# A two-layer hybrid mixer on one core: the Fourier branch takes its position transform first and in half, and unused columns move where operand rows begin

## The chip, the cores and the metric

The kernel runs on one core of a Trainium2 chip. The metric is the device time of one execution in microseconds. Beside it stands one profiled execution, whose span runs from its first instruction to its last. Lower is better.

## The reference

Two layers work on two sequences of 256 tokens with 1024 channels: the latent tokens and the context tokens. Each layer normalises and modulates its input, multiplies it by one wide input matrix, and feeds three token mixers. Branch A is a Fourier mixing, branch B a gated delta rule run forwards and backwards over chunks, branch C a differential attention. Each branch is projected back to 1024 channels and gated, the three are summed, one output matrix follows, and then a squared-ReLU MLP of width 4096. Layer 0 carries both sequences; in layer 1 only the latent tokens go on after the keys, values and states, so most of its products have 256 columns where those of layer 0 have 512.

The part that the change is about is this:

```
def fourier_mix(u):                      # u: (batch, t, 512)
    uf = u.reshape(b, t, 4, 128)         # 4 groups of 128 channels
    y = fft2(uf, axes=(1, 3), norm='ortho').real
    return y.reshape(b, t, 512)
y_f = fourier_mix(h @ w_in[:, 0:512]) @ w_f
```

With C and S the cosine and sine matrices, the real part for one group is C_pos u C_ch - S_pos u S_ch. The cosine over positions is even and the sine is odd, so position 256 - t repeats position t up to a sign.

## The kernel before

**Products.** All large products take float32 operands split in two rounded halves (`split`, L257: a ScalarE copy gives the high half, a VectorE subtraction the low half) and are three matmuls each (`mm3`, L241): high by high, low by high, high by low. `gemm` (L246) runs `mm3` over eight blocks of 128 input channels into one PSUM bank: a chunk of 128 x 1024 weights is stationary, block by block, and the tokens move, 512 or 256 columns at a time. A chunk is thus 24 matmuls. `load_w` (L226) fetches a chunk by a SyncE DMA, copies it on ScalarE and subtracts on VectorE (`whi`, `wlo`).

**Layer.** `mixer` (L448) calls in order: `front` (modulation of the input, and products that start while it runs), `dn_pair(0)` (q, k, v products of two delta-rule heads and their convolution), `fnet` (the Fourier branch), `scores` and `values` (attention inputs), `branch` for the Fourier projection and its gate, the attention, the chain of head pair 0, and then the same for pair 1, the other gates and projections, and the merge. `accumulate` (L1116) does the output matrix (`C_WO`) and the second MLP matrix. `mlp` (L1156) writes the squared hidden values as the pair `a`.

**Order of the work.** The delta-rule chain of small dependent matmuls is written out after the products, and `weave.chain()` places its instructions among those already written, by their planned TensorE time. Beyond that, instructions are put on each engine in order of priority as they become ready, so a product that stands later in the code can run ahead where a PSUM bank is free. There are eight banks, two each under the tags `pg`, `pa`, `pc` and `pd`; the chain uses `pc` and `pd`. Within `fnet` a product may use `pg` alone.

**`fnet` before (L880).** Channel-major: for each of the four groups, one chunk gives u (128 channels x n tokens; n is 512 in layer 0, 256 in layer 1). It is split, each tile of 128 tokens is stationary against the 128 x 256 table `cc` (both channel transforms), the result z is split, and then z is stationary against the position table `ct` (256 columns), over two token tiles and over cosine and sine. The result is split into `yb`. Group 0 of layer 0 is computed already in `front0` (L1280).

**Where operand rows begin.** A tile's columns lie one after another in each partition. The rows of the operands below are 1024 or 2048 bytes apart, so all rows of one operand begin at the same byte modulo 512. From the allocation:

| moving operand | columns of a matmul | bytes mod 512, layer 0 | layer 1 |
|---|---|---|---|
| `hh`, `hl` (input of all products) | 512 or 256 | 288, 288 | 288, 288 |
| `a0`, `a1` (MLP hidden values) | 512 (layer 0), 256 (layer 1) | 288, 352 | 480, 480 |
| `yh`, `yl` (Fourier, then attention output) | 512, 256 | 480, 480 | 480, 480 |
| `ydh`, `ydl` (delta-rule output) | 512, 256 | 128, 128 | 64, 64 |
| `ct`, `cc` (transform tables) | 256 | 224 | 128 |
| weight chunks `whi`, `wlo` | (128 when stationary) | 288 | 288 |

Of the kernel before, what the change touches and what calls it, by code (L numbers as in the profile page):

```python
# [30 lines left out]
NLVL = 7  # L31

# [47 lines left out]
def constants():  # L80
# [89 lines left out]
def body(tc, A, dbg=None):  # L170
# [12 lines left out]
    hh = [hp.tile([P, KT, T], F32R, name=t_) for t_ in ("hh", "hl")]  # L183
# [23 lines left out]
    def abank():  # L207
        return bank("pa")
# [43 lines left out]
    def step_of(jobs, k, t0, n, order=range(KT), X=hh):  # L252
# [72 lines left out]
    def lambdas(pool):  # L325
        lamv = wp.tile([P, 1024], F32, tag="raw", name="raw", bufs=4)[:, 0:R_END - R_LAM]
        nc.gpsimd.dma_start(lamv, A["rows"][R_LAM:R_END].partition_broadcast(P))
        lamv = lamv.rearrange("p (a b c) -> p a b c", a=DEPTH, b=4)
        for l in range(DEPTH):
            lj = pool.tile([P, 2, 64], F32, name=f"lj{l}")  # L330
# [104 lines left out]
    def modulate(l, x, r, a, base, s, k, pool, eng=V):  # L435
        sl = slice(s * L, (s + 1) * L)
        t = pool.tile([P, L], F32, tag="mt", name="mt", bufs=3)
        hi, lo = hh[0][:, k, sl], hh[1][:, k, sl]
# [9 lines left out]
    def mixer(l, last, front):  # L448
# [3 lines left out]
        H = hh  # L452
# [427 lines left out]
        def fnet():  # L880
# [4 lines left out]
            cr = raw_tile(A["ct"])  # L885
            ct = [fp.tile([P, 1024], F32R, name=f"ct{i}") for i in range(2)]
            split(cr, ct[0], ct[1])
            ct = [c_.rearrange("p (k c) -> p k c", k=2) for c_ in ct]
            cc = [fp.tile([P, 256], F32R, name=f"cc{i}") for i in range(2)]
            split(raw_tile(A["kc"][:, K_CC:K_CC + 256], 256), cc[0], cc[1])  # L890
            nt = n // P
            for g in range(4):
                ps = product(("u", g), C_U + g, n)
                uh = [fp.tile([P, n], F32R, tag=f"uh{i}", name=f"uh{i}", bufs=2) for i in range(2)]
                split(ps[:, :n], uh[0], uh[1])
                z = [fp.tile([P, nt, 256], F32R, tag=f"z{i}", name=f"z{i}") for i in range(2)]
                for tt in range(nt // 2):
                    pz = abank()
                    for i in range(2):
                        t = 2 * tt + i  # L900
                        tk = slice(t * P, (t + 1) * P)
                        mm3(pz[:, i * 256:(i + 1) * 256], uh[0][:, tk], uh[1][:, tk], cc[0], cc[1], True, True)
# [561 lines left out]
```

## Time and profile before

| | |
|---|---|
| median of 3 runs | 1619.63 us (1617.7 to 1624.81) |
| the profiled execution's own time | 1620.69 us |
| its span | 1618.9 us |
| TensorE busy | 1541.4 us, 95% of the span, 10270 matmuls |
| VectorE busy | 1183.2 us, 73% |
| ScalarE busy | 738.9 us, 46% |
| granted TensorE clock, mean | 0.990 |

The busy time of TensorE (PE) is modelled from starts, since matmuls overlap, so the page alone doesn't tell how fast a stream of them runs. For that one takes the start of the first and the last matmul of an unbroken run and divides by their number. PEld is the weight load that goes ahead of each matmul; DVE is VectorE and ACT is ScalarE.

### The profile page before, as it was taken

How to read it: one execution, taken by the hardware profiler on the slowest of the kernel's cores; microseconds unless marked ns; L12 is line 12 of the kernel's file. 1: busy time of each engine (PE TensorE's matmuls, PEld its weight loads, DVE VectorE, ACT ScalarE, POOL GpSimd, SP SyncE). 2: the span in 40 equal slices, each digit the busy share in tenths (PEclk: the TensorE clock that was granted, in tenths of full speed). 3: DMA queues.
4: the chain of work that ended last, by engine and by line, in shares of the span. 5: the costliest groups of instructions: out<-in, count | busy, mean ns of one | idle time of the engine just before them, and what ended most of it. 6: DMA issues, size and time to landing. Idle time of an engine off the chain costs nothing.

```text
span 1618.9 us, 26446 instructions
## 1 busy us (share of the span) xinstructions
PE 1541.4 (95%) x10270; PEld 1327.9 (82%) x10270; DVE 1183.2 (73%) x2221; ACT 738.9 (46%) x1525; POOL 187.9 (12%) x196
## 2 busy tenths in 40 slices
PE   5889999999999999999999999899999999999997
PEld 2568888778787878788888888788988899999997
DVE  7686665767789867967767664876877885887765
ACT  3465543566542233422223233465547554555543
POOL 3420100011002103000000004211111102000001
PEclk9999999999999999999999999899999999999998
DMA  6522123211166635466656552231332125656662
GB/s 234 186 89 66 34 66 117 90 54 38 48 196 202 219 127 200 130 196 195 182 182 196 173 171 82 70 121 60 93 117 79 41 89 177 186 170 192 189 185 91
DMA packets 64462, 215.85 MB, mean 133 GB/s; under 512 B 7281, under 2 KB 12305, under 8 KB 64081
## 3 DMA queue, kind: packets, MB, share of 16 engines
q1 hardware_dynamic: 58178, 202.48, 39.8%
q10 hardware_dynamic: 5184, 7.21, 1.3%
q0 software_dynamic: 976, 4.48, 0.9%
q8 instruction: 80, 1.31, 0.3%
q14 instruction: 44, 0.36, 0.1%
HBM read 209.95 MB, written 4.20 MB: 132 GB/s over the span
## 4 chain that ended last, share of the span: by engine, by line
PE 73%; DVE 15%; ACT 5%; issue 3%; DMA 3%; POOL 0%; DVEq 0%; ACTq 0%; SPq 0%; POOLq 0%
PE pg L146 35%; PE pd L146 13%; PE pa L146 12%; PE pc L146 11%; DVE junk L319 3%; DVE cy L614 2%; DVE wlo L238 2%; DMA raw<-in_wt 2%; ACT whi L237 1%; DVE mt L440 1%; ACT sw L952 1%; PE pc L154 1%; PE pa L154 1%; DMA wv<-in_wt 0%; DMA x<-in_xin 0%
## 5 line engine op out<-in xcount | busy, mean ns | idle before, releaser
L238 DVE TENSOR_TENSOR wlo<-raw,whi 128x1024 fp32r<-128x1024 f32 x262 | 326.4, 1246 | 99.1 <-ACT whi L237 96.5
L237 ACT CAST whi<-raw 128x1024 fp32r<-128x1024 f32 x277 | 290.1, 1049 | 223.2 <-PE pg L146 79.7
L146 PE MATMUL pg<-hh,whi 128*128 128x512 f32 (+1 forms) x912 | 324.7, 356 | 1.8 <-DVE gt L876 1.8
L146 PE MATMUL pg<-hh,wlo 128*128 128x512 f32 (+1 forms) x912 | 323.9, 355 | 2.0 <-POOL wlo L238 1.5
L146 PE MATMUL pg<-hl,whi 128*128 128x512 f32 (+1 forms) x912 | 323.2, 354 | 0.0
L146 PEld LDWEIGHTS pg<-hh,whi 128*128 128x128 f32 x912 | 172.6, 189 | 23.7 <-issue 3.1
L319 DVE CUSTOM_DVE_ANT_0 junk<-raw,cb 128x1024 f16<-128x1024 f32 x128 | 160.4, 1253 | 41.8 <-DMA raw<-in_wt 38.2
L146 PEld LDWEIGHTS pg<-hh,wlo 128*128 128x128 f32 x912 | 172.7, 189 | 22.0 <-POOL wlo L238 1.8
L146 PEld LDWEIGHTS pg<-hl,whi 128*128 128x128 f32 x912 | 173.0, 190 | 20.7 <-issue 0.8
L417 POOL TENSOR_TENSOR acc<-acc,sq 128x256 f32<-128x256 f32 x36 | 38.9, 1088 | 596.3 <-ACT sq L415 596.3
L146 PE MATMUL pg<-a,whi 128*128 128x256 f32 (+1 forms) x416 | 102.0, 328 | 0.1
L614 DVE SCALAR_TENSOR_TENSOR cy<-cu,conv,cy 128x512 f32<-128x512 f32 (+1 forms) x96 | 75.7, 789 | 30.9 <-ACT cy L612 28.5
L146 PEld LDWEIGHTS pg<-a,whi 128*128 128x128 f32 x416 | 70.7, 188 | 8.4 <-DVE a L259 0.5
L860 ACT ACTIVATE gt<-pg 128x512 f32<-128x512 f32 (+1 forms) x44 | 21.6, 491 | 114.6 <-PE pg L146 100.8
L146 PE MATMUL pg<-a,wlo 128*128 128x256 f32 (+1 forms) x208 | 68.0, 327 | 0.0
L146 PE MATMUL pc<-a,whi 128*128 128x512 f32 (+1 forms) x224 | 57.2, 336 | 0.1
L146 PE MATMUL pd<-a,whi 128*128 128x256 f32 (+1 forms) x224 | 54.7, 328 | 0.0
L1186 DVE TENSOR_TENSOR mr<-mr 128x512 f32<-128x512 f32 (+1 forms) x64 | 35.4, 555 | 25.3 <-ACT mr L1185 25.2
L740 ACT CAST Um<-pd 128x512 f16<-128x512 f32 x56 | 34.1, 610 | 35.8 <-PE pd L146 35.3
L146 PE MATMUL pa<-a,whi 128*128 128x256 f32 (+1 forms) x208 | 50.0, 324 | 0.1
L146 PE MATMUL pa<-hh,whi 128*128 128x512 f32 (+1 forms) x128 | 48.3, 377 | 0.0
L146 PE MATMUL pa<-hl,whi 128*128 128x512 f32 (+1 forms) x128 | 48.1, 376 | 0.0
(435 smaller groups left out, 3675.3 us busy)
## 6 DMA issues: line engine op xcount, KB each, us to landing
raw<-in_wck SPq DMA_DIRECT2D x280, 512.0 KB, 3.6
raw<-in_wt SPq DMA_DIRECT2D x80, 512.0 KB, 3.6
wv<-in_wt SPq DMA_DIRECT2D x10, 512.0 KB, 4.2
wn<-in_wn SPq DMA_DIRECT2D x16, 192.0 KB, 3.8
x<-in_xin SPq DMA_DIRECT2D x4, 512.0 KB, 8.6
spill<-gt ACTq DMA_DIRECT2D x8, 256.0 KB, 4.0
cb<-crow POOLq DMA_DIRECT2D x2, 1024.0 KB, 5.8
merged<-spill ACTq DMA_DIRECT2D x8, 256.0 KB, 4.4
```

Of the source, the lines that this page charges most:

```text
L146: ins = self.pe.matmul(out, a, b, start=start, stop=stop)
L154: self.pe.transpose(out, a, ident)
L237: S.copy(hi, r)
L238: eng.tensor_tensor(out=lo, in0=r, in1=hi.bitcast(F32), op=ALU.subtract)
L319: V.tensor_tensor_reduce(out=junk, in0=r, in1=self.cb[:, v], scale=0.5, scalar=0.0, op0=ALU.mult, op1=ALU.add, accum_out=ada[l][:, n, v:v ...
L417: G.tensor_tensor(out=self.acc[s], in0=self.acc[s], in1=q, op=ALU.add)
L440: V.scalar_tensor_tensor(out=t, in0=x[s][:, k], scalar=gain, in1=r[s], op0=ALU.mult, op1=ALU.mult)
L614: V.scalar_tensor_tensor(out=y3, in0=u[:, 0:ns, j:j + L], scalar=conv[:, f, j:j + 1], in1=y3, op0=ALU.mult, op1=ALU.add)
L740: S.copy(uc_, pU.rearrange("p (d b c) -> p d b c", d=2, c=w_))
L860: S.activation(th, ps[:, :n], AF.Tanh, scale=0.5)
L952: S.copy(sw[b:b + 32], ps[b ^ 32:(b ^ 32) + 32, 0:L])
L1186: V.tensor_tensor(out=t, in0=t, in1=t, op=ALU.mult)
```

## The change

`fnet` works on token-major data. The four chunks of u's weights are laid out by input channel, so that now the tokens are stationary (128 of them) and 512 weight columns move; n/128 banks (4 in layer 0, 2 in layer 1) hold u for all groups at once. A unit is one group of one sequence: 8 in layer 0, 4 in layer 1. Two units at a time, `positions` multiplies u by a table of 256 columns that holds 129 cosines and 127 sines in place of 512 columns, and after a split `channels` applies cosine and sine of the channels to the two halves, with `cc` stationary and z moving (260 and 256 columns). The sine part is copied in reverse to the second half of y on ScalarE, VectorE subtracts it for positions 1 to 127 and adds it for their mirror images, and y is split into `yb`. In `front0` the chunk of u that was computed early is replaced by gate chunk (C_GF, 1).

The second part are columns that nothing uses. `hh` is made 48 columns wider and `hl` 80: layer 0 uses `hh` from column 0 and `hl` from column 80, layer 1 `hh` from column 48 and `hl` from 0. The two make 128 columns, 512 bytes, so what lies behind keeps its byte modulo 512. `pad` allocates 48 columns behind `yb` in layer 0 (its pool grows downwards), 40 and 104 columns ahead of `yd` in layers 0 and 1, and 112 ahead of `a1` in layer 0. By these sums rows begin at 288 for `hh`, `hl`, `a0`, `a1`, `yb` and `yd` in layer 0, and at 480 for all of them in layer 1. `lambdas` puts a scratch product into a weight buffer in place of two tiles of its own.

```
--- before.py
+++ after.py
+NC = L // 2 + 1
-    ct = np.concatenate([np.cos(a) / 16, -np.sin(a) / 16], axis=1).astype(np.float32)
-    ct = ct.reshape(2, P, 512).transpose(1, 0, 2).reshape(P, 1024)
+    ct = np.concatenate([np.cos(a[:, 0:NC]) / 16, np.sin(a[:, 1:NC - 1]) / 16], axis=1).astype(np.float32)
+    ct = ct.reshape(2, P, L).transpose(1, 0, 2).reshape(P, 2 * L)
+SHIFT = ((0, 48), (80, 0))
+PAD = {"y": (48, 0), "yd": (40, 104), "a": ((0, 112), (0, 0))}
+def pad(pool, w):
+    if w:
+        pool.tile([P, w], F32, name="pad")
-    hh = [hp.tile([P, KT, T], F32R, name=t_) for t_ in ("hh", "hl")]
+    hs = [[], []]
+    for t_, at_ in zip(("hh", "hl"), SHIFT):
+        t = hp.tile([P, KT * T + max(at_)], F32R, name=t_)
+        for l_ in range(DEPTH):
+            hs[l_].append(t[:, at_[l_]:at_[l_] + KT * T].rearrange("p (k c) -> p k c", c=T))
...
-            cr = raw_tile(A["ct"])
-            ct = [fp.tile([P, 1024], F32R, name=f"ct{i}") for i in range(2)]
-            split(cr, ct[0], ct[1])
+            ct = [fp.tile([P, 2 * L], F32R, name=f"ct{i}") for i in range(2)]
+            split(raw_tile(A["ct"], 2 * L), ct[0], ct[1])
...
-            for g in range(4):
-                ps = product(("u", g), C_U + g, n)
...
+            ps = [bank("pg") if t < 2 else bank("pa") for t in range(nt)]
+            for c in range(4):
+                w = [w_.rearrange("p k c -> p (k c)") for w_ in load_w(l, C_U + c)]
+                for i in range(2):
+                    k, cols = 2 * c + i, slice(512 * i, 512 * i + 512)
+                    for t in range(nt):
                         tk = slice(t * P, (t + 1) * P)
-                        mm3(pz[:, i * 256:(i + 1) * 256], uh[0][:, tk], uh[1][:, tk], cc[0], cc[1], True, True)
...
+                        mm3(ps[t], H[0][:, k, tk], H[1][:, k, tk], w[0][:, cols], w[1][:, cols], k == 0, k == KT - 1)
+            u = [fp.tile([P, nt, 512], F32R, name=f"u{i}") for i in range(2)]
+            for t in range(nt):
+                split(ps[t], u[0][:, t], u[1][:, t])
+            units = [(g, s) for g in range(4) for s in range(nseq)]
+            def positions(i):
+                pq = bank("pg").rearrange("p (a c) -> p a c", a=2)
+                for j, (g, s) in enumerate(units[i:i + 2]):
+                    gs = slice(g * P, (g + 1) * P)
                     for k in range(2):
+                        mm3(pq[:, j], u[0][:, 2 * s + k, gs], u[1][:, 2 * s + k, gs], ct[0][:, k], ct[1][:, k], k == 0, k == 1)
+                return pq
+            def channels(i, z):
+                pa_, pb_ = (abank()[:, :2 * w_].rearrange("p (a c) -> p a c", a=2) for w_ in (NC + 1, NC - 1))
+                mm3(pa_, cc[0][:, 0:P], cc[1][:, 0:P], z[0][:, :, 0:NC + 1], z[1][:, :, 0:NC + 1], True, True)
+                mm3(pb_, cc[0][:, P:2 * P], cc[1][:, P:2 * P], z[0][:, :, NC - 1:L], z[1][:, :, NC - 1:L], True, True)
+                y = fp.tile([P, 2, L], F32, tag="y", name="y")
+                sn = y[:, :, L - 1:NC - 1:-1]
+                S.copy(y[:, :, NC:L], pb_[:, :, NC - 2:0:-1])
+                S.copy(y[:, :, 0:NC:NC - 1], pa_[:, :, 0:NC:NC - 1])
+                V.tensor_tensor(out=y[:, :, 1:NC - 1], in0=pa_[:, :, 1:NC - 1], in1=sn, op=ALU.subtract)
+                V.tensor_tensor(out=sn, in0=pa_[:, :, 1:NC - 1], in1=sn, op=ALU.add)
+                g = units[i][0]
+                hi, lo = (t[:, g:g + 2] if last else t[:, g].rearrange("p (a c) -> p a c", a=2) for t in yb)
+                split(y, hi, lo)
+            pq = positions(0)
+            for i in range(0, len(units), 2):
+                z = [fp.tile([P, 2, L], F32R, tag=f"z{j}", name=f"z{j}") for j in range(2)]
+                split(pq, z[0], z[1])
+                if i + 2 < len(units):
+                    pq = positions(i + 2)
+                channels(i, z)
...
         yb = [yp.tile([P, 4, n], F32R, name=t_) for t_ in ("yh", "yl")]
+        pad(yp, PAD["y"][l])
...
+        pad(tp, PAD["yd"][l])
         yd = [tp.tile([P, 4, n], F32R, name=t_) for t_ in ("ydh", "ydl")]
...
+            a = []
+            for i in range(2):
+                if q == 0:
+                    pad(pool, PAD["a"][l][i])
+                a.append(pool.tile([P, KT, n], F32R, tag=f"a{i}", name=f"a{i}", bufs=2))
...
-                          lambda: job(("u", 0), load_w(0, C_U, pair(st, "wu"), G), "pa"),
+                          lambda: job((C_GF, 1), load_w(0, C_GF + 1, pair(st, "wu"), G), "pa"),
...
-        wck[l, C_U:C_U + 4] = pack(w[:, 0:512])
+        wck[l, C_U:C_U + 4] = w[:, 0:512].reshape(4, 2, P, 512).transpose(0, 2, 1, 3).reshape(4, P, 1024)
```

## Rows read from the trace of the kernel before

**Rows 1.** The page, parts 1 and 2, whole execution.

```profile
PE 1541.4 (95%) x10270; PEld 1327.9 (82%) x10270; DVE 1183.2 (73%) x2221; ACT 738.9 (46%) x1525; POOL 187.9 (12%) x196
PEclk9999999999999999999999999899999999999998
```

**Rows 2.** The page, part 4: the chain that ended last, by engine.

```profile
PE 73%; DVE 15%; ACT 5%; issue 3%; DMA 3%; POOL 0%; DVEq 0%; ACTq 0%; SPq 0%; POOLq 0%
```

**Rows 3.** Stretches: us; PE, PEld, DVE, ACT, POOL busy us (instructions); clock; DMA share; GB/s.

```profile
128.00:178.00 50.00, 49.96 (x445) 43.27 (x443) 34.68 (x72) 28.76 (x65) 3.62 (x3) 1.00 0.15 46
1009.00:1058.00 49.00, 40.54 (x292) 37.32 (x291) 42.09 (x96) 23.81 (x56) 18.39 (x19) 0.90 0.22 68
1058.00:1108.00 50.00, 48.97 (x404) 44.92 (x402) 37.51 (x84) 35.00 (x86) 3.36 (x5) 1.00 0.40 126
1108.00:1340.00 232.00, 222.19 (x2007) 197.67 (x2005) 182.49 (x409) 131.65 (x316) 30.06 (x35) 1.00 0.26 80
1370.00:1423.00 53.00, 52.91 (x446) 52.71 (x445) 41.58 (x67) 28.71 (x49) 5.65 (x6) 1.00 0.60 188
667.00:1003.00 336.00, 336.00 (x1525) 277.54 (x1524) 224.97 (x329) 100.89 (x140) 11.56 (x11) 1.00 0.56 174
```

**Rows 4.** One tile's instructions: `z`, then `uh`; ns min/median/max, first and last start us.

```profile
L146 PE MATMUL pa<-ct,z x144: 277/282/388, 131.2 to 1105.1; 128*128 128x256 f32 x144
...
L146 PE MATMUL pa<-cc,uh x72: 276/283/386, 128.3 to 1099.8; 128*128 128x256 f32 x72
```

**Rows 5.** Timeline of PE, `hh`/`hl` by 256 columns, layer 1: start, us.

```profile
1400.19 0.28 PE L146 MATMUL pc<-hh,wlo 128*128 128x256 f32 x1
...
1422.99 0.28 PE L146 MATMUL pd<-hl,whi 128*128 128x256 f32 x1
```

**Rows 6.** Timeline of PE, `hh`/`hl` by 512 columns, layer 0.

```profile
741.13 0.39 PE L146 MATMUL pd<-hh,whi 128*128 128x512 f32 x1
...
784.46 0.39 PE L146 MATMUL pa<-hl,whi 128*128 128x512 f32 x1
```

**Rows 7.** Groups by line and form, 128 to 178 us: busy us, mean ns; ACT, then DVE.

```profile
L258 ACT CAST z<-pa 128x512 fp32r<-128x512 f32 x8 | 4.8, 594 | 2.5 <-PE pa L146 2.3
...
L259 DVE TENSOR_TENSOR z<-pa,z 128x512 fp32r<-128x512 f32 x8 | 5.4, 686 | 0.1
...
L727 DVE TENSOR_TENSOR X<-pd,lvl 128x512 f16<-128x512 f32 x7 | 4.8, 687 | 3.4 <-PE pd L146 3.4
L736 DVE TENSOR_TENSOR Tm<-pd,Tm 128x512 f16<-128x512 f32 x6 | 4.1, 690 | 1.9 <-PE pd L146 1.7
...
L712 DVE TENSOR_TENSOR dec<-dec,gq 128x256 f32<-128x256 f32 x4 | 1.5, 417 | 0.0
```

**Rows 8.** Timeline of PE, `yh`/`yl` by 512 columns, layer 0.

```profile
589.77 0.39 PE L146 MATMUL pg<-yh,whi 128*128 128x512 f32 x1
...
597.93 0.39 PE L146 MATMUL pg<-yl,whi 128*128 128x512 f32 x1
```

**Rows 9.** Timeline of PE, `a0`/`a1` by 512 columns, layer 0.

```profile
784.69 0.39 PE L146 MATMUL pg<-a,whi 128*128 128x512 f32 x1
...
828.99 0.39 PE L146 MATMUL pd<-a,whi 128*128 128x512 f32 x1
```

**Rows 10.** Timeline of PE, `ydh`/`ydl` by 512 columns in layer 0, by 256 in layer 1.

```profile
511.74 0.40 PE L146 MATMUL pg<-ydh,whi 128*128 128x512 f32 x1
...
516.89 0.39 PE L146 MATMUL pg<-ydh,wlo 128*128 128x512 f32 x1
...
1359.14 0.28 PE L146 MATMUL pg<-ydh,whi 128*128 128x256 f32 x1
...
1361.74 0.28 PE L146 MATMUL pg<-ydh,wlo 128*128 128x256 f32 x1
```

**Rows 11.** Timeline of PE, `a0`/`a1` by 256 columns, layer 1.

```profile
1451.96 0.28 PE L146 MATMUL pa<-a,wlo 128*128 128x256 f32 x1
...
1469.77 0.28 PE L146 MATMUL pg<-a,whi 128*128 128x256 f32 x1
```

More of the change, by code (lines that the diff above doesn't have):

```diff
@@ L250, in gemm, with step_of @@
         return ps
-    def step_of(jobs, k, t0, n, order=range(KT), X=hh):
+    def step_of(jobs, k, t0, n, order=range(KT), X=hs[0]):
         for ps, w, m in jobs:
@@ L325, in lambdas @@
     def lambdas(pool):
-        lamv = wp.tile([P, 1024], F32, tag="raw", name="raw", bufs=4)[:, 0:R_END - R_LAM]
+        raw = wp.tile([P, 1024], F32, tag="raw", name="raw", bufs=4)
+        lamv, ljs = raw[:, 0:R_END - R_LAM], raw[:, R_END - R_LAM:].rearrange("p (a b c) -> p a b c", a=DEPTH, c=64)
         nc.gpsimd.dma_start(lamv, A["rows"][R_LAM:R_END].partition_broadcast(P))
@@ L329, in lambdas @@
         for l in range(DEPTH):
-            lj = pool.tile([P, 2, 64], F32, name=f"lj{l}")
+            lj = ljs[:, l]
             le = pool.tile([P, 2], F32, name=f"le{l}")
@@ L437, in modulate @@
         t = pool.tile([P, L], F32, tag="mt", name="mt", bufs=3)
[L438 removed]
+        hi, lo = hs[l][0][:, k, sl], hs[l][1][:, k, sl]
         gain, shift = a[:, k, s:s + 1], ada[l][:, base + k, s:s + 1]
@@ L451, in mixer @@
         lam_init = LAM_INIT[l]
-        H = hh
+        H = hs[l]
         ex = ExitStack()
@@ L891, in fnet @@
             nt = n // P
-            for g in range(4):
-                ps = product(("u", g), C_U + g, n)
[L894 to L900, printed above, removed]
-                        tk = slice(t * P, (t + 1) * P)
-                        mm3(pz[:, i * 256:(i + 1) * 256], uh[0][:, tk], uh[1][:, tk], cc[0], cc[1], True, True)
-                    split(pz.rearrange("p (a b) -> p a b", a=2), z[0][:, 2 * tt:2 * tt + 2], z[1][:, 2 * tt:2 * tt + 2])
-                pm = abank()
-                for s in range(nseq):
-                    for k in range(2):
-                        for c in range(2):
-                            cs = slice(c * P, (c + 1) * P)
-                            mm3(pm[:, s * L:(s + 1) * L], z[0][:, 2 * s + k, cs], z[1][:, 2 * s + k, cs],
-                                ct[0][:, k, c * 256:(c + 1) * 256], ct[1][:, k, c * 256:(c + 1) * 256],
-                                k == 0 and c == 0, k == 1 and c == 1)
-                split(pm[:, :n], yb[0][:, g], yb[1][:, g])
@@ L1032, in mixer @@
         front(mp, dp, job, gate_weights)
-        show(f"h{l}", hh[0].bitcast(F32))
+        show(f"h{l}", H[0].bitcast(F32))
         yp = ex.enter_context(tc.tile_pool(name="yp", bufs=1, side="right", reuse_waits="tile"))
         yb = [yp.tile([P, 4, n], F32R, name=t_) for t_ in ("yh", "yl")]
+        pad(yp, PAD["y"][l])
         conv = mp.tile([P, 12, 5], F32, name="conv")
@@ L1164, in mlp @@
         else:
-            H, m = hh, n
+            H, m = hs[l], n
             ma = pool.tile([P, 8, 2], F32, name="ma")
@@ L1174, in mlp @@
         for q in range(4):
-            a = [pool.tile([P, KT, n], F32R, tag=f"a{i}", name=f"a{i}", bufs=2) for i in range(2)]
+            a = []
[3 more added lines that the diff above has]
+                a.append(pool.tile([P, KT, n], F32R, tag=f"a{i}", name=f"a{i}", bufs=2))
             for j in range(KT):
@@ L1361, in front1 @@
                 modulate(1, x1, r1, ma, 0, s, k, cp_)
-                step_of(jobs, k, s * L, L)
+                step_of(jobs, k, s * L, L, X=hs[1])
             if s == 0:
```

4 lines of the change are left out of this document (2 added, 2 removed).

## The prediction

> **What bounds the kernel now.** I read the page first. TensorE is busy for 95% of the span with nine tenths or more of its full clock granted in all but two of forty slices [rows 1], and the chain that ended last lies on it for 73% [rows 2]. Then I read stretches. In the MLP of layer 0 it is busy for 336 of 336 us, in the output matrix of layer 1 for 52.9 of 53, around `fnet` for 49.96 of 50 in layer 0 and 48.97 of 50 in layer 1. In the rest of layer 1's mixer it is 222.2 of 232, and only the front of layer 1, where the modulation sets the pace, leaves much open: 40.5 of 49 [rows 3]. So a matmul that goes saves its start-to-start spacing nearly everywhere, and so does a spacing that shrinks. Last I read the spacing itself, run by run, from the first and last start of unbroken streams.
>
> **Fourier branch, matmuls.** Before, layer 0 runs 240 matmuls (96 of 512 columns for u, 48 with `cc`, 96 with `ct`), layer 1 168 (96 of 256 columns for u, 24, 48); the trace has 72 and 144 of the last two kinds [rows 4]. After, layer 0 runs 96 of 512 columns, 48 for `positions` (8 units x 2 blocks x 3) and 24 for `channels` (4 pairs x 6): 168. Layer 1 runs 48 + 24 + 12 = 84. A 256-column matmul costs 120.0 ns: 191 starts from 1400.19 to 1422.99, 190 spacings [rows 5]; I price the 260 columns of `channels` the same. Layer 0 saves 72 x 0.120 = 8.6 us. Layer 1 saves 36 x 0.120 = 4.3, and its u goes from 96 x 0.120 = 11.5 to 48 x 0.2269 = 10.9 (512 columns: 192 starts from 741.13 to 784.46 [rows 6]), 0.6 more: 4.9. The early chunk in the front is swapped for another of 24 matmuls, and one chunk fewer is left to `dn_pair(0)`: nothing, since both stand in the count above. No DMA is added; the table shrinks.
>
> **Fourier branch, new waits.** Before, TensorE ran ahead: while a group was split, the next group's u filled in, and there was no idle time in 128 to 178 us [rows 3]. After, u comes as one block that holds both `pg` banks (in layer 0 both `pa` banks as well), and what follows is short and dependent. Behind the last u matmul, a ScalarE copy of 0.59 and a VectorE subtraction of 0.69 [rows 7] stand before the last token tile may be used. The earlier tiles are split by then, so of that 1.3 us plus handovers about 1 us is idle. Then each pair needs copy, subtraction, and the assembling of y. The next pair's `positions` (12 x 0.120 = 1.44 us) covers the split, and `channels` is 0.72. For VectorE a pair is 0.69 twice and two half-wide operations (the 256-column one took 0.42 [rows 7]): 2.2 us, as long as TensorE's 2.16. For ScalarE it is 0.59 twice and two small copies, for which no row stands: each between 0.2 and 0.59, I take 0.4, the nearest being half of the full copy and a fixed part: 2.0 us. The chain of head pair 0 is woven into the same stretch and puts two VectorE operations of 0.69 into every level [rows 7]. Per pair, VectorE then has more work than TensorE, until `scores` gets a freed `pg` bank and fills in. Bounds: in layer 0 from 0.5 us (the tail of the last split alone) to 8 (each of four pairs exposes a copy, a subtraction and one chain operation, 2.0 us); I take 3.0. In layer 1, with two pairs, from 0 to 4; I take 1.7. ScalarE and VectorE have no less to do over `fnet` than before, only bunched. `lambdas` and the shorter table save a microsecond of VectorE where TensorE doesn't wait for it: nothing.
>
> **Unused columns.** In stretches where the granted clock was 1.00 (2.4 GHz) [rows 3] the streams differ by operand, with the same kind of stationary operand at the same place. At 512 columns: `hh`/`hl`, beginning at 288 modulo 512, 226.9 ns [rows 6]; `yh`/`yl` at 480, (597.93 - 589.77)/35 = 233.1 [rows 8]; `a0`/`a1` at 288 and 352, (828.99 - 784.69)/191 = 231.9 [rows 9]; `ydh`/`ydl` at 128, (516.89 - 511.74)/22 = 234.1 [rows 10]. At 256 columns the order is reversed: `hh`/`hl` at 288 120.0 [rows 5], `a0`/`a1` at 480 (1469.77 - 1451.96)/157 = 113.4 [rows 11], `ydh`/`ydl` at 64 (1361.74 - 1359.14)/22 = 118.2 [rows 10]. I read this as the place of the row's beginning, as the change does: it puts every operand of layer 0 to 288, best of the four at 512, and every one of layer 1 to 480, best of the three at 256. Terms:
> - `a` in layer 0: 696 matmuls of 512 columns (768 less the halved last three chunks) x 5.0 ns = 3.5 us.
> - `yb` in layer 0: two projections of 96 x 6.2 = 1.2 us. In layer 1 it stays.
> - `yd`: 96 x 7.2 = 0.7 in layer 0, 96 x 4.8 = 0.5 in layer 1.
> - `hh` in layer 1 at 256 columns: 1200 matmuls (front 144, q of the delta rule 96, three gates 576, z 96, attention q 96, output matrix 192) x 6.6 = 7.9 us if all count. The 144 of the front do not, since TensorE waits there. In 1108 to 1340 us I count seven tenths of what lies in it, because with 10 us idle some of the gain only lengthens waits for the chain. I take 5.0; bounds 2.1 (output matrix and the gates next to it) and 7.9.
> - `hh` in layer 1 at 512 columns (k and v of the delta rule less two early, attention k: 240) go from 226.9 to 233.1: 1.5 us lost.
> Should the place not matter at all, the four gains and the loss are nought; no row shows one operand at two places.
>
> The Trainium skill speaks against this part. "TensorE: Matmul & The Clock Gate", section "Back-to-back issue gap", gives the spacing by the number of columns alone, N/2.4 + 2.5 ns, so 215.8 and 109.2 wherever a row begins; and "SBUF — State Buffer", section "Operand start alignment", calls alignment a matter of legality and says that its runs timed nothing. The trace disagrees with one number per width: 226.9 to 234.1 and 113.4 to 120.0 at full granted clock. By the rule the padding would give nothing, which is the first rival below.
>
> **Sum.** -8.6 - 4.9 + 3.0 + 1.7 - 3.5 - 1.2 - 1.2 - 5.0 + 1.5 = -18.2 us, against the profiled execution's own 1620.69: 1602.5. That execution stands 1.1 above the median of the runs, 1619.63, so the forecast is 1601.5.
>
> **Rivals.**
> - *The place does not matter* (the streams differ by layer or tile for another reason): only the branch counts, -8.6 - 4.9 + 4.7 = -8.8, 1610.8. For it: each place is also another tile. Against: at each width the three or four streams sort by place, and none needs another cause. Chance 0.10.
> - *Layer 1's mixer runs at the pace of its chain*: the matmuls saved there (3.2 net of the branch, 3.7 of `hh`) come back as waits for the recurrence; with the loss at 512 columns hidden as well, about 6 us less gain, 1608. For it: 10 us of idle in 232 and VectorE busy for 182 [rows 3]. Against: TensorE is still at 96% there. Chance 0.15.
> - *The pairs run in series, slower than before*: y, z and the chain's operations queue on VectorE so that `positions` no longer covers them. A pair then takes copy 0.59, subtraction 0.69, `channels` 0.72, six operations for y (0.4, 0.4, 0.42, 0.42, 0.59, 0.69) and two of the chain, 1.4: 6.3 us with 2.2 of TensorE work in it. Six pairs leave 25 us idle and the two ends of u 5 more: 30 against the 4.7 I count, 1627. It decides from 22.9 us idle on, where all gains are used up. For it: VectorE is the second busiest engine and takes its work in order. Against: `scores` can run ahead from the third pair on. Chance 0.05.
> - *Everything is hidden and everything counts*: no idle, 7.9 for `hh`: -25.8, 1594. Chance 0.08.
>
> **How the numbers follow.** The forecast has 0.62. Its own terms move it between 1597 and 1607. The range 1592 to 1612 takes in the first, second and fourth rival and leaves out the third and the tails. Half a percent, about what a measurement of this kernel can tell from no change, is 8.1 us: faster means below 1611.5. The forecast and the fourth rival give nearly all of 0.70, the second 0.12, the first, which lies at the line, 0.05; allowing for a cause that I do not see, 0.84. Slower: 0.04. The rest, 0.12, is no change.
>
> **What would show it.** TensorE has 156 matmuls fewer, 10114. Streams of `a`, `yh`, `ydh` in layer 0 run at 227 ns, those of `hh` in layer 1 at 113 to 114 by 256 columns and 233 by 512; a stream that keeps its old spacing proves that step wrong, and 120 for `hh` in the output matrix of layer 1 would be the plainest sign. The MLP of layer 0 gets 3.5 us shorter, the stretch of `fnet` in layer 0 about 5.6. Idle time of TensorE before `positions` and `channels`, with VectorE or ScalarE as what ended it, sums to about 3 us in layer 0; above 9 my price of the new waits is wrong. The prediction fails if idle time grows elsewhere, most of all in 1058 to 1340 us.

## The result, and the profile after

| | before | after |
|---|---|---|
| median of the runs made side by side | 1618.66 us (4 runs, 1616.62 to 1624.81) | 1601.31 us (4 runs, 1597.02 to 1601.53) |
| ratio | | 0.9881, 95% interval 0.9865 to 0.9897 |
| the profiled execution's own time, its span | 1620.69, 1618.9 | 1601.47, 1599.7 |

The forecast was 1601.5. The total came out as forecast, and two of its terms did not: the Fourier branch was worth nearly twice what I gave it, the unused columns about half. First the page after, parts 1, 2 and 4:

```profile
PE 1520.1 (95%) x10114; PEld 1307.5 (82%) x10114; DVE 1175.1 (73%) x2224; ACT 735.9 (46%) x1527; POOL 187.1 (12%) x195
...
PEclk9999999999999999999999999899999999999998
...
PE 69%; DVE 18%; ACT 5%; issue 4%; DMA 3%; POOL 0%; DVEq 0%; ACTq 0%; POOLq 0%
```

The matmuls are 10114, as forecast, 156 fewer than in [rows 1]; TensorE's busy time fell by 21.3 us and the span by 19.2. Its share of the chain that ended last went from 73% [rows 2] to 69%, VectorE's from 15% to 18%. Where there were 144 and 72 matmuls on `z` and `uh` [rows 4] there are now 72 and 36. Two tiles of the kernel after, `ct` and then `cc` (columns as in [rows 4]):

```profile
L158 PE MATMUL pg<-ct,u x72: 274/283/388, 147.3 to 1080.9; 128*128 128x256 f32 x72
```

```profile
L158 PE MATMUL pa<-z,cc x36: 277/284/388, 151.8 to 1084.8; 128*128 128x260 f32 x18, 128*128 128x256 f32 x18
```

The spacings, from the first and the last start of unbroken streams in the timeline of the kernel after: `a` in layer 0 (192 starts), `yh`/`yl` in layer 0 (36), `hh`/`hl` by 256 columns in layer 1 (171).

```profile
772.36 0.39 PE L158 MATMUL pc<-a,whi 128*128 128x512 f32 x1
...
815.65 0.39 PE L158 MATMUL pg<-a,whi 128*128 128x512 f32 x1
...
578.33 0.39 PE L158 MATMUL pg<-yh,whi 128*128 128x512 f32 x1
...
586.26 0.39 PE L158 MATMUL pg<-yl,whi 128*128 128x512 f32 x1
...
1383.56 0.28 PE L158 MATMUL pd<-hh,whi 128*128 128x256 f32 x1
...
1402.84 0.28 PE L158 MATMUL pa<-hl,whi 128*128 128x256 f32 x1
```

That is 226.6 ns for `a` (231.9 in [rows 9]), 226.6 for `yh` (233.1 in [rows 8]) and 113.4 for `hh` (120.0 in [rows 5]). So in this execution the streams did what the prediction said. The stages did not all follow. The table cuts the span at certain TensorE starts (the same instructions in every kernel): us of each stage, and in brackets TensorE's idle time in it, counted as the excess of start-to-start times over the usual spacing of that width, which takes in time lost at the lower clock too. The kernels of the other columns are told of below.

| stage | before | after | branch alone, twice | columns alone | after, no rows | branch alone, no rows |
|---|---|---|---|---|---|---|
| start to the first convolution | 98.8 (42.8) | 97.7 (41.8) | 98.3, 100.5 | 97.7 | 98.3 | 97.6 |
| to the Fourier projection, layer 0 | 121.7 (11.8) | 110.7 (9.8) | 110.6, 110.7 | 123.2 (13.2) | 110.7 | 110.7 |
| Fourier projection and what runs beside it | 59.8 (2.7) | 60.7 (3.4) | 61.1, 61.1 | 59.3 | 60.7 | 61.1 |
| to the first `ydh` | 198.3 (21.4) | 198.1 (21.1) | 198.0, 198.0 | 198.1 | 198.2 | 198.3 |
| first `ydh` to last `yl` | 119.4 (9.1) | 119.1 (10.1) | 115.6 (5.3), 115.7 (5.5) | 118.5 (9.6) | 108.8 (0.1) | 110.3 (0.1) |
| output matrix, layer 0 | 98.7 | 98.7 | 99.1, 99.0 | 98.4 | 98.7 | 99.8 |
| MLP, layer 0 | 312.8 (3.2) | 310.9 (4.8) | 312.9, 313.1 | 309.3 (3.3) | 309.5 (3.5) | 314.6 (4.9) |
| front of layer 1 to its Fourier projection | 134.1 (24.6) | 128.0 (24.8) | 128.9, 129.0 | 135.0 (26.7) | 128.4 | 128.8 |
| to the first `ydh` of layer 1 | 196.1 (25.9) | 198.3 (27.9) | 197.1 (26.1), 197.1 (26.2) | 195.9 (26.8) | 198.4 (28.0) | 197.1 (26.1) |
| to the last `yl` | 60.5 | 58.9 | 60.5, 60.5 | 59.7 | 58.9 | 60.5 |
| to the end | 218.8 | 218.6 | 219.4, 218.8 | 218.4 | 218.7 | 218.8 |

### The profile page after: what moved, and what is told of

It reads as the page before. It is cut to its first block, busy times and chain, and to the rows that moved or that the text cites. A ratio compares the mean times of both kernels' runs of the same rounds, so it can differ in the third digit from the quotient of the medians.

```text
span 1599.7 us, 26147 instructions
## 1 busy us (share of the span) xinstructions
PE 1520.1 (95%) x10114; PEld 1307.5 (82%) x10114; DVE 1175.1 (73%) x2224; ACT 735.9 (46%) x1527; POOL 187.1 (12%) x195
## 4 chain that ended last, share of the span: by engine, by line
PE 69%; DVE 18%; ACT 5%; issue 4%; DMA 3%; POOL 0%; DVEq 0%; ACTq 0%; POOLq 0%
PE pg L158 35%; PE pd L158 13%; PE pa L158 11%; PE pc L158 10%; DVE junk L336 3%; DVE wlo L255 3%; DVE cy L632 3%; DMA raw<-in_wt 2%; ACT whi L254 1%; DVE mt L458 1%; ACT sw L995 1%; PE pa L166 1%; PE pc L166 1%; DMA rows<-in_rows 0%; DMA wv<-in_wt 0%
## 5 line engine op out<-in xcount | busy, mean ns | idle before, releaser
L158 PE MATMUL pg<-hh,whi 128*128 128x512 f32 (+1 forms) x856 | 304.1, 355 | 0.9 <-DVE gt L894 0.7
L158 PE MATMUL pg<-hl,whi 128*128 128x512 f32 (+1 forms) x856 | 303.3, 354 | 0.0
L158 PE MATMUL pg<-hh,wlo 128*128 128x512 f32 (+1 forms) x856 | 302.7, 354 | 0.6 <-DVE wlo L255 0.6
L158 PEld LDWEIGHTS pg<-hl,whi 128*128 128x128 f32 x856 | 163.0, 190 | 19.3 <-issue 0.8
L158 PEld LDWEIGHTS pg<-hh,wlo 128*128 128x128 f32 x856 | 162.6, 190 | 19.0 <-DVE wlo L255 0.7
L878 ACT ACTIVATE gt<-pg 128x256 f32<-128x256 f32 (+1 forms) x43 | 21.0, 488 | 99.1 <-PE pg L158 82.2
L158 PE MATMUL pd<-a,whi 128*128 128x512 f32 (+1 forms) x224 | 56.7, 334 | 0.1
L158 PE MATMUL pa<-hh,wlo 128*128 128x512 f32 (+1 forms) x152 | 53.9, 355 | 0.0
L158 PE MATMUL pg<-whi,hh 128*128 128x256 f32 (+1 forms) x160 | 51.0, 319 | 0.7 <-DVE q L996 0.5
L158 PE MATMUL pg<-wlo,hh 128*128 128x256 f32 (+1 forms) x160 | 50.1, 314 | 0.0
```

What stands on the lines that cost most here:

```text
L158: ins = self.pe.matmul(out, a, b, start=start, stop=stop)
L878: S.activation(th, ps[:, :n], AF.Tanh, scale=0.5)
```

## The experiments

My theory after the result: the terms of the prediction hold one by one, and the place of a row's beginning sets the spacing. Rivals: the place has nothing to do with it; or the two parts have other worths that happen to add up.

**The places by themselves.** The kernel leaves the model out and only streams matmuls of float32 halves at chosen beginnings; 48 of them end in one bank.

```
+ for cols in (512, 256):
+     for p in list(range(0, 128, 8)) + list(range(120, -1, -8)):
+         run(cols, p)             # 16 x (high by high, low by high, high by low); rows begin p columns in
+ ... the low half elsewhere than the high half; steps under 8 columns; the stationary rows moved
```

> This kernel leaves the whole model out: it only streams split-float32 matmuls from one pair of operands, 48 at a time, with the row's beginning moved in steps of 32 bytes through 512, by 512 and by 256 columns, twice each, then in steps of 4 to 16 bytes, with the two operands at different places, and with the stationary operand moved. Theory (the place of the row's beginning modulo 512 bytes sets the spacing): 512 columns take 226 to 228 ns at 288 and 233 to 234 at 480, 256 columns 119 to 120 at 288 and 113 to 114 at 480, with the same operands throughout, and each step reads the same on the second pass. Rival (the spacing belongs to the operand or the stage): one spacing for each width, within 1 ns, at all places.

A ScalarE copy follows each 48 matmuls, so the copies' starts give the mean spacing. The timeline of ScalarE, at 512 columns: up to the second copy the moving rows begin 448 bytes behind the stationary ones, up to the last three 320, then 288, then 256:

```profile
237.21 0.16 ACT L206 COPY o<-pg 128x1 f32<-128x1 f32 x1 [11.04 <-PE pg L205]
248.41 0.16 ACT L206 COPY o<-pg 128x1 f32<-128x1 f32 x1 [11.04 <-PE pg L205]
...
282.02 0.16 ACT L206 COPY o<-pg 128x1 f32<-128x1 f32 x1 [11.04 <-PE pg L205]
293.02 0.16 ACT L206 COPY o<-pg 128x1 f32<-128x1 f32 x1 [10.84 <-PE pg L205]
304.21 0.16 ACT L206 COPY o<-pg 128x1 f32<-128x1 f32 x1 [11.03 <-PE pg L205]
315.12 0.16 ACT L206 COPY o<-pg 128x1 f32<-128x1 f32 x1 [10.75 <-PE pg L205]
```

11.20 us over 48 are 233.3 ns; 11.00, 11.19 and 10.91 are 229.2, 233.1 and 227.3. Over all places in steps of 32 bytes, what counts is how far the moving row begins behind the stationary one, modulo 256: at 0 the spacing is 227 by 512 columns and 120 by 256; at 64 it is 229 and 113 to 118, at 192 (the 448 above) 233 and 114 to 118 (by 256 columns two passes over the same place differed); elsewhere 232 to 234 and 117 to 120. Moving the stationary rows instead gave the same numbers by 512 columns, 226.7 at distance 0 and 229.3 at 64. So neither rival nor theory as it was worded: the place modulo 512 alone is not the rule. In the model the weights always begin at 288, so the place 288 of the prediction is distance 0, and 480 is 192. For these two the theory's numbers came in the streams as in the kernel: 227 and 120 at 288, 233 and 114 at 480, but 118 in the first pass.

**Columns alone, and branch alone.**

```
 columns alone = before, with
+SHIFT = ((0, 48), (80, 0))
+PAD = {"y": (48, 0), "yd": (40, 104), "a": ((0, 112), (0, 0))}
 branch alone = after, with
-SHIFT = ((0, 48), (80, 0))
-PAD = {"y": (48, 0), "yd": (40, 104), "a": ((0, 112), (0, 0))}
+SHIFT = ((0, 0), (0, 0))
+PAD = {"y": (0, 0), "yd": (0, 0), "a": ((0, 0), (0, 0))}
```

> The kernel before with the unused columns alone, Fourier branch as before. Theory (place): the terms of the forecast for the columns, 3.5 + 1.2 + 1.2 + 5.0 - 1.5 = 9.4 us less, 1609; the stage between the first Fourier projection and the first delta-rule projection of layer 1 gains nothing or loses a little, because waits take it back, so 1609 to 1612. Rival (the columns do nothing): 1618.5.

> The changed kernel with all unused columns at zero, so the new Fourier branch alone. Theory (place): forecast 8.8 us less than before, 1609.9; if the branch's new waits are covered, as the profile of the changed kernel suggests, up to 12 less, 1606.5. Rival (the columns do nothing): as the changed kernel, 1601.3.

Measured beside a before of 1619.95: columns alone 1614.59 (ratio 0.9965, 0.9954 to 0.9975), 5.4 us; branch alone 1602.32 (0.9893, 0.9875 to 0.9912), 17.6 us. The forecast had 9.4 and 8.8. Both times lie outside what I had expected of these runs: columns alone above 1612, branch alone below 1606.5 and near the 1601.3 of the rival that the columns do nothing, which columns alone rule out. The two gains add up to 23, and the whole change gives 17 to 24 by its own repeats, so the sum of the forecast was right with both terms wrong.

**Places swapped** (layer 0 at 480, layer 1 at 288, the branch kept).

```
-SHIFT = ((0, 48), (80, 0))
-PAD = {"y": (48, 0), "yd": (40, 104), "a": ((0, 112), (0, 0))}
+SHIFT = ((48, 0), (0, 80))
+PAD = {"y": (0, 48), "yd": (88, 56), "a": ((0, 112), (80, 0))}
...
+        ml0.tile([P, 48], F32, name="padr")
```

> The changed kernel with the two places exchanged: all operands of layer 0 at 480, all of layer 1 at 288. Theory (place): layer 0 loses 2016 x 6.2 ns (hh by 512) + 696 x 6.5 (a) + 288 x 6.3 (y, yd) and gets back 384 x 6.3 (256 columns); layer 1 loses 1200 x 6 x 0.7 + 768 x 6.4 + 192 x 5, gets back 1.5: 12.5 + 4.5 + 1.8 - 2.4 + 5.0 + 4.9 + 1.0 - 1.5 = 26 us more than the changed kernel, about 1627. Rival (the spacing belongs to the operand): 1601.3, and every stream keeps its spacing.

1613.94 (ratio 0.9967, 0.9955 to 0.9979), 12.6 us above the median of the kernel after, or 14 by the two ratios, since each has its own runs of the kernel before. That is half of the 26 that I expected. The stream of `a` in layer 0, 192 starts of the timeline:

```profile
776.66 0.39 PE L158 MATMUL pc<-a,whi 128*128 128x512 f32 x1
...
821.23 0.40 PE L158 MATMUL pg<-a,whi 128*128 128x512 f32 x1
```

233.4 ns. `hh` by 256 columns in layer 1 went back to 120.0. The same instructions in the same order, with only the beginnings moved, change the spacing and the time: this settles that the place is a cause. The MLP is 7.6 us longer than after, the last stage 4.3 and the output matrix 2.0. But the three stages from the first convolution to the first `ydh` are together only 2 us longer, and from the first `ydh` to the last `yl` the kernel is 2.3 us shorter, at 116.8, although its streams there are the slower ones. That stage is the odd one.

**The kernel after once more.**

> The changed kernel unaltered, timed in more rounds, to price the unused columns on the new branch (against the run of the branch alone, ratio 0.9893 of before). If the columns are worth what they are worth on the old branch (ratio 0.9965, 5.7 us), 0.9858, 1597; if waits take most of them back here, 0.988 to 0.989, 1601 to 1602.

1597.38 (5 runs, 1594.77 to 1604.37; ratio 0.9861, 0.9840 to 0.9882). The profiled execution was the slowest of the five, 1604.37. It has 121.2 us between first `ydh` and last `yl`, with 12.1 idle; 10.2 us of that stage are at the clock's lower level, 1.2 GHz, where the kernel after has 3.4. And one stream has another spacing, though the granted clock is 1.00 in both: the same 171 starts of `hh`/`hl` by 256 columns in the output matrix of layer 1.

```profile
1386.39 0.28 PE L159 MATMUL pd<-hh,whi 128*128 128x256 f32 x1
...
1406.41 0.28 PE L159 MATMUL pa<-hl,whi 128*128 128x256 f32 x1
```

That is 117.8 ns, where the kernel after had 113.4. The next experiment has 118 here too; the later chain, no look-ahead and the kernel without rows, all told of below, have 113.4. So distance 192 gives one of two spacings by 256 columns. What decides between them was not tried.

**`gh`/`gl` at one place.** The rows of these two tiles are 1032 bytes apart, so each begins at another place; here all begin at distance 192.

```
-            self.h = [pool.tile([P, KT, L + 2], F32R, name=t_) for t_ in ("gh", "gl")]
+            pool.tile([P, 32], F32, name="padg")
+            self.h = [pool.tile([P, KT, 320], F32R, name=t_)[:, :, 0:L + 2] for t_ in ("gh", "gl")]
```

> The changed kernel, in which also the input rows of layer 1's first MLP matrix (gh, gl; 258 columns, 1032 bytes apart, so that each row began elsewhere) are 1280 bytes apart and begin at 480 and 224 in turn, 192 modulo 256 behind the stationary rows at 288. Theory (the distance of the moving row's beginning from the stationary row's, modulo 256 bytes, sets the spacing): the 768 matmuls go from 120 ns to about 114.5 (258 columns), 4.2 us less than the changed kernel, since TensorE is busy all through that stage: 1597. Rival (the place modulo 512 counts): the rows at 224 stay near 120, 2.1 us less. Rival (the weight supply bounds the stage): spacing falls, time does not.

1599.44 (ratio 0.9874, 0.9856 to 0.9891). The 768 matmuls of 258 columns have a median spacing of 120.0 in both kernels, and the stage that holds them, to the end, 219.3 us against 218.6; these 0.7 are the output matrix at 118 ns. So the place that gives 113 to 118 by 256 columns gives nothing by 258.

**What hides the branch's waits.** Two covers were taken away. In the first the next pair's `positions` shares its banks with the pair that is being split, so it can't start ahead. In the second the chain of head pair 0 starts 32 us of planned time later, so it isn't woven into `fnet`.

```
-                pq = bank("pg").rearrange("p (a c) -> p a c", a=2)      # in positions: a bank of its own
+            pq = [bank("pg") for _ in range(2)]                         # once, for all pairs
...
-                dn_chain(p, q2, k2, ktm, vtm, now[0] + POST[1], lat)
+                dn_chain(p, q2, k2, ktm, vtm, now[0] + POST[1] + (32.0 if l == 0 and p == 0 else 0.0), lat)
```

> The changed kernel, in which positions writes two banks that are held, one unit in each, so the next pair's positions cannot start before the split of this pair is done. Theory A (positions of the next pair covers the split): each pair after the first exposes copy, subtraction and handover, 1.5 us, in layer 0 three and in layer 1 one: idle time of the branch grows by 6 us, 1607. Theory B (the woven chain of head pair 0 covers it): under 2 us more, 1602 to 1603.

> The changed kernel, in which the chain of head pair 0 of layer 0 is placed 32 us of TensorE work later, behind the Fourier branch. Theory B (the chain covers the branch's waits): idle time in layer 0 from the last u matmul to the last channels matmul rises from under 1 us to 3 or more. Theory A (lookahead covers them): idle stays under 1.5 us and the stretch just loses the chain's own matmuls, which come back later. Time 1600 to 1605 by either, as the chain has to run somewhere.

Without the banks of their own: 1602.44 (0.9888, 0.9874 to 0.9901), and the stage up to the Fourier projection 112.7 us with 12.0 idle, against 110.7 with 9.8. That is 2 us, not the 6 of theory A. With the chain later: 1602.95 (0.9888, 0.9869 to 0.9906), and from the first convolution to the first `ydh` 371.5 us against 369.5. But these 2 us are not lost in the branch. From the last u matmul to the last of `channels`, with the chain later and then in the kernel after (columns as in [rows 3]):

```profile
143.70:158.40 14.70, 14.70 (x105) 13.62 (x104) 10.21 (x19) 8.13 (x18) 0.00 (x0) 1.00 0.13 43
```

```profile
146.70:164.10 17.40, 16.76 (x205) 14.70 (x204) 16.31 (x29) 10.27 (x22) 0.16 (x1) 1.00 0.12 31
```

Without the chain TensorE never waits there, as theory A has it; theory B wanted 3 us of idle time or more. Behind the branch, up to the end of the Fourier projection, its waits are 1.9 us against 0.4. So the chain is not what covers the branch. The timeline of that stretch has `positions` of later pairs and other products between the matmuls of `channels`. Taking look-ahead and chain away together was not tried. Neither run shows in the whole time: the intervals overlap that of the kernel after. Even without look-ahead TensorE's idle time in the two stages around `fnet` is 15.4 us, 0.9 above before, where I had charged 3.0.

**The odd stage.** Between first `ydh` and last `yl` of layer 0 the kernel also computes 24 rows of the modulation for later: VectorE multiplies each by `cb` as its DMA lands (`junk`). The waits in that stretch after, VectorE's and then TensorE's:

```profile
DVE junk L336 <- DMA raw<-in_wt: 9.9, 6, 3.3
```

```profile
PE pg L158 <- DVE gt L894: 7.3, 4, 3.0
```

`gt`, which empties the `pg` bank, stands on VectorE behind products of rows, and TensorE waits for `gt`. Two of the four waits, in the timeline of the kernel after:

```profile
506.95 1.23 DVE L336 CUSTOM_DVE_ANT_0 junk<-raw,cb 128x1024 f16<-128x1024 f32 x1
508.10 0.68 DVE L894 SCALAR_TENSOR_TENSOR gt<-gt,pg 128x512 f32<-128x512 f32 x1
508.84 0.59 PE L158 MATMUL pg<-ydh,whi 128*128 128x512 f32 x1 [2.98 <-DVE gt L894]
...
542.68 1.23 DVE L336 CUSTOM_DVE_ANT_0 junk<-raw,cb 128x1024 f16<-128x1024 f32 x1 [2.21 <-DMA raw<-in_wt]
543.83 0.68 DVE L894 SCALAR_TENSOR_TENSOR gt<-gt,pg 128x512 f32<-128x512 f32 x1
544.57 0.50 PE L158 MATMUL pg<-yh,whi 128*128 128x512 f32 x1 [2.98 <-DVE gt L894]
```

In the first case VectorE had worked through four products of rows without a pause; in the second it had waited 2.2 us for a row. The first wait is in every profile with rows, 1.8 to 3.0 us. The second is in all seven with the columns at these places or at distance 64, 0.3 to 3.0 us, and not in those of the kernel before, of the branch alone or of the swapped places. Before, the two lines of waits read 8.5 and 5.3; with the branch alone (second run) 6.1 and 3.4. If the rows set the pace here, a faster stream only waits longer. The two kernels without these rows, and two more beside them:

```
-            aw = Rows([(0, i, 2) for i in range(16, 40)], cond_rows(tp), tp)
+            aw = Rows([], cond_rows(tp), tp)
+            V.memset(ada[0][:, 16:40], 0.0)
```

> The changed kernel without the 24 modulation rows that are computed between the first ydh and the last yl of layer 0 (their DMA and their products are left out and their place is filled with zeros, so the output is another). In that stretch the changed kernel took 119.05 us with 10.1 idle, the branch alone 115.55 with 5.3, and the kernel before 119.43 with 9.1. Theory: the rows' DMA sets that stretch's end, so the narrower spacings there (192 of yh by 6.2 ns and 96 of ydh by 7.2: 1.9 us) only lengthened waits. Without the rows idle falls below 3 us here, and the stretch is 1.5 to 2 us shorter than in the branch alone without rows. Rival: the stretch is at the pace of something else (vector work on the gates); idle stays at 5 or more without the rows and the two kernels differ by under 0.7 us there. For the whole kernel, theory: 5 to 7 us below r2_no_rows_branch; rival: 1 to 4 us, as the changed kernel stands to the branch alone.

> The branch alone (no unused columns), without the same 24 modulation rows (they are left out in the same way). Theory: idle below 3 us between the first ydh and the last yl of layer 0, where with the rows it was 5.3, and that stretch 1.5 to 2 us longer than in r1_no_rows. Rival: idle of 5 us or more in it, and no difference to r1_no_rows.

> The branch alone once more, unaltered, beside the three others on the same chip. Theory: 1 to 4 us above the changed kernel in the whole (1602.32 against 1601.31 and 1597.38 before), with the stretch between the first ydh and the last yl of layer 0 anywhere between 115 and 120 us, since what it waits for there is a DMA. Rival: the stretch comes to 115.5 us again, so the unused columns made it slower.

Without rows: after 1591.49 (0.9815, 0.9799 to 0.9832), branch alone 1599.22 (0.9868, 0.9855 to 0.9882). With them, the branch alone again: 1604.41 (0.9903, 0.9889 to 0.9917). The stretch itself, after and branch alone, both without rows (us; then busy time and instructions of PE, PEld, DVE, ACT, POOL; granted clock; DMA share; GB/s):

```profile
467.90:576.70 108.80, 108.80 (x481) 89.91 (x480) 47.22 (x51) 32.12 (x41) 10.84 (x9) 1.00 0.36 110
```

```profile
467.70:578.00 110.30, 110.30 (x480) 89.84 (x479) 47.71 (x52) 32.13 (x41) 10.32 (x8) 1.00 0.32 99
```

TensorE is busy throughout, and the columns' 1.5 us are there; the 1.9 I expected had counted the 96 `yh` of the Fourier projection too, which lies outside; the two streams in the stretch are 96 x 6.2 + 96 x 7.2 ns, 1.3. The same stretch with rows, after and branch alone:

```profile
467.20:586.30 119.10, 111.82 (x483) 90.75 (x482) 99.67 (x135) 32.45 (x41) 18.21 (x9) 0.99 0.59 193
```

```profile
470.30:586.00 115.70, 112.26 (x482) 91.06 (x481) 99.68 (x136) 32.37 (x41) 17.66 (x8) 0.99 0.59 190
```

There VectorE has 52 us more to do and the DMA moves 190 GB/s instead of 100 to 110. For the whole kernel the columns are worth 7.7 us without the rows and, measured side by side, 4.2 with them (1604.41 against 1600.22 for the kernel of the next experiment, which differs from the one after in one place). The theory stands: the rows take the columns' gain of this stage. One expectation went the rival's way: with rows the branch alone came to 115.7 again, below the 117 to 121 us of all six profiles that have branch, columns and rows (distance 64 among them; the swapped places have 116.8). Why faster streams make this stage longer, and not merely no shorter, I did not settle. Removing the rows removes the difference, but it takes away both their DMA and 52 us of VectorE's work, and which of the two costs the time was not tried apart.

**A place in between.** `hh` and `hl` of layer 1 at distance 64.

```
-SHIFT = ((0, 48), (80, 0))
+SHIFT = ((0, 16), (80, 32))
```

> The changed kernel with hh and hl of layer 1 beginning at 352 instead of 480 modulo 512, that is 64 bytes instead of 192 behind the place of the weights modulo 256; nothing else moves. Theory (the spacing follows the distance between the two rows' beginnings modulo 256): as where the streams were measured by themselves at that distance, 512 columns at 229 to 229.5 ns (233 to 234 at 480), 256 columns at 113 to 118 (114 at 480). Some 246 matmuls of 512 columns gain 4.5 ns: 1.1 us; some 1160 of 256 lose 0 to 4 ns: 0 to 4.6 us where TensorE does not wait. Time 1597 to 1605, no measurable change. Rival (the place modulo 512 alone): 352 is where a1 began in layer 0 before, 231.9 ns by 512 columns mixed with a0 at 288, so 236 to 237 for 352 alone, slower than at 480.

1600.22 (0.9876, 0.9859 to 0.9893). Timeline, `hh`/`hl` of layer 1 by 512 columns (29 starts), then by 256 (169):

```profile
1189.03 0.39 PE L158 MATMUL pg<-hh,whi 128*128 128x512 f32 x1
...
1195.43 0.40 PE L158 MATMUL pg<-hh,wlo 128*128 128x512 f32 x1
...
1384.20 0.28 PE L158 MATMUL pd<-hh,whi 128*128 128x256 f32 x1
...
1403.99 0.28 PE L158 MATMUL pa<-hh,whi 128*128 128x256 f32 x1
```

228.6 and 117.8 ns: both as the distance modulo 256 says, and the first against the 236 of the place modulo 512. The 117.8 are no different from the repeat's at distance 192. (By this edit `hl` begins at 96 modulo 512, not at 352 as `hh` does; modulo 256 both are at distance 64.) The stage to the last `yl` of layer 1 is 59.9 us against 58.9, and the time is that of the kernel after.

## Why the prediction was right and wrong

**Right: the counts and the spacings.** The matmuls are the 10114 forecast. Every stream took the spacing that I read for its place from another tile: `a` and `yh` 227, `hh` in layer 1 113 to 114 by 256 columns and 233 by 512; in two of the six profiles with the branch and these places, the output matrix had 118. The rule that I read, the place modulo 512, is not the rule: it gave these numbers because the weights of this kernel all begin at one place.

**Wrong: "Fourier branch, new waits".** This is the step that failed in the branch. I charged 3.0 us in layer 0 and 1.7 in layer 1. From the first convolution to the end of the Fourier projection the branch alone is 9.6 us shorter than before (171.8 against 181.4), with 1.3 less idle, not 3.0 more; the 72 matmuls that went are 8.6 of it. The timeline of the kernel after shows why, in the middle of `fnet`:

```profile
151.04 0.59 ACT L275 CAST z<-pg 128x512 fp32r<-128x512 f32 x1 [1.68 <-PE pg L158]
151.10 1.22 DVE L255 TENSOR_TENSOR wlo<-raw,whi 128x1024 fp32r<-128x1024 f32 x1
151.32 0.30 PEld L158 LDWEIGHTS <-Tm 128*128 128x128 f16 x8
151.32 0.42 PE L158 MATMUL pd<-id,Tm 128*128 128x64 f16 x8
...
151.81 0.72 PE L158 MATMUL pa<-z,cc 128*128 128x260 f32 x4
...
152.83 0.68 DVE L276 TENSOR_TENSOR z<-pg,z 128x512 fp32r<-128x512 f32 x1
152.97 0.39 PE L158 MATMUL pd<-X,Um 128*128 128x64 f16 x8 [0.43 <-DVE X L745]
...
153.56 0.51 PE L158 MATMUL pa<-z,cc 128*128 128x260 f32 x2 [0.21 <-DVE z L276]
...
153.91 0.52 PE L158 MATMUL pg<-ct,u 128*128 128x256 f32 x3
```

`channels` starts on the high half, the chain's matmuls go in while VectorE is still at `wlo`, `channels` finishes on the low half after 0.21 us of waiting, and the next `positions` follows. I had set the chain down as a rival for VectorE that leaves the branch bare. A rival it is, since these two waits are gone where the chain runs later, but one of 0.6 us and not 3.0: `positions` of the next pair and other products are ready meanwhile. All waits for z, X and `ktm` in `fnet` of layer 0 sum to 0.8 us after, and a wait of 2.1 us for the gate chain (`g`) that stood before the Fourier projection is gone. Taking the look-ahead away cost 2 us, taking the chain away nothing within the branch. In layer 1 the front and the Fourier part are 4.2 us shorter with the branch alone (326.0 against 330.2), with 0.6 more idle where I charged 1.7.

**Not forecast: 3.8 us between first `ydh` and last `yl`** with the branch alone (115.6 against 119.4). The matmuls there are the same. TensorE waits 3.4 us for `gt` and not 5.3, and 3.4 us of the stage are at the 1.2 GHz level and not 6.8, by estimate 1.7 us at half the clock: with the 1.9 us of waits most of the 3.8. The columns take it away again. With these the branch makes 9.6 + 4.2 + 3.8 = 17.6 us, what the first run measured; the second gave 15.9.

**Wrong: "Unused columns", the worth.** Of the 9.4 us I forecast, the whole kernel shows 5.4 added alone, about 4 on top of the branch (17.4, 24.1 and, at distance 64, 20.1 below before, against 17.6 and 15.9), and 7.7 on top of it without the rows. Term by term: `a` 3.5 forecast, 3.6 by its spacing (161.4 to 157.8 us of TensorE), and the MLP is 3.5 shorter with columns alone (1.9 in the kernel after, where 3.4 us of it have a granted clock of 0.50). `yb` and `yd` of layer 0, 1.9 forecast: 0.5 appears at the Fourier projection, the rest in the stage of the rows, where it is lost. `hh` in layer 1 by 256 columns, 5.0 forecast with 7.9 as its bound: 1.2 in the output matrix as forecast (the stage to the end shows 0.2 to 0.8 of it), 1.6 from the first `ydh` to the last `yl` of layer 1, `yd` included; but in the stage up to that `ydh` the 504 matmuls of 256 columns with `hh` (in 96 of them it is the stationary operand) went, waits left out, from 60.5 to 59.1 us, 2.8 ns each and not 6.6. I put that down to the short matmuls of the chain among which they stand, which was not tried. With the 0.7 lost by 512 columns there (40.0 to 40.7 us) 0.7 is left. And the stage is 1.2 us longer, not shorter. The clock takes more than that gain (timeline cut in stretches, columns as above; after, then the branch alone):

```profile
1180.00:1184.90 4.90, 2.89 (x15) 2.24 (x14) 3.91 (x3) 1.62 (x3) 2.05 (x3) 1.00 0.29 107
1184.90:1188.30 3.40, 3.40 (x18) 3.40 (x17) 2.76 (x5) 2.38 (x10) 0.00 (x0) 0.51 0.00 0
```

```profile
1183.00:1188.00 5.00, 2.92 (x14) 2.25 (x12) 4.15 (x4) 1.37 (x3) 2.40 (x3) 1.00 0.32 95
1188.00:1191.50 3.50, 3.46 (x28) 3.42 (x29) 2.87 (x5) 2.76 (x11) 0.00 (x0) 1.00 0.04 14
```

Both kernels wait here for `cy`, 2 us. After it the clock of the kernel after is 0.51, the 1.2 GHz level, for 3.4 us, and 18 matmuls go in 3.4 us where 28 go in 3.5 at 2.4 GHz. Of the profiles with branch and columns five have this stretch (the kernel after, its repeat, the later chain, the one without rows, distance 64), two have not (`gh` at one place with 196.8 us for the stage, no look-ahead with 195.5), and none of the three of the branch alone has it; the swapped places have it too. The wait for `cy` before it is 1.8 to 2.1 us in all of them, so it alone does not decide. What does was not tried.

**The rivals.** "The place does not matter" fell with the swapped places. "Layer 1's mixer runs at the pace of its chain" was half right: of the columns' gain up to the first `ydh` nothing came through, but because of the clock and the small gain per matmul and not of new waits, while the branch's gain came through but for 0.6 us. "In series" did not happen. The sum was right because 7 to 9 us too little for the branch stood against about 5 too much for the columns (its terms give 1601.4, and 1601.5 is a rounding). That is luck, but for the stage of the rows, where the columns lose what the branch gains.

**What the Trainium skill says.** "TensorE: Matmul & The Clock Gate", section "Back-to-back issue gap", gives spacings by the width alone; the formula that the prediction took from it is there for an isolated matmul, beside about 131 ns for a stream of 512 columns. The swapped places, one program in two layouts, give 227 and 233 ns for one stream at 2.4 GHz, so here the measurement decides against one number per width. "SBUF — State Buffer", section "Operand start alignment", says of its own runs that they timed nothing; no row here is against that.

## What to carry to other kernels

Before charging waits to a short dependent sequence, list what else may run on the bound engine at that moment: look-ahead with a bank of its own, and other products that were ready, left 0.8 us where I had charged 3.0. A spacing that shrinks is worth its count times nanoseconds only in stages where the bound engine never waits; in the others, take the work away that it waits for (here 8.7 us when the rows are left out, measured beside distance 64; they are needed, so moving them may give less) before polishing the stream. And test both parts of a two-part change apart, even when the total is as forecast. A second profile of the same kernel is worth having too: here it showed another spacing and another clock in two stages.

## What the runs showed of the hardware

- The spacing of float32-half matmuls depends on how far the moving rows begin behind the stationary ones, modulo 256 bytes: by 512 columns 227 ns at 0, 229 at 64, 232 to 234 at the other steps of 32, 192 among them; by 256 columns 120 at 0 and at 96, 113 to 118 at 64 and 192, 117 to 119 else. By 256 columns one place can give two spacings at a granted clock of 1.00: at 192 113.4 in one execution of a kernel and 117.8 in another, in the streams alone 117.8 and 114.0.
- Off the 32-byte steps: 4 bytes off 236 to 237 (512 columns) and 123 (256); by 512 columns 8 bytes 233 to 234, 16 bytes 231.5 to 231.7. With the high half at distance 0 and the low half at 64 it was 231.9, just what `a` had before [rows 9].
- By 258 columns the spacing stayed at 120 whether rows began at 16 places or at one.
